# Up projection: product 2 of two neighbouring pairs as seven half-size products, and the next pair's product 1 sooner

## The chip, the cores and the metric

The kernel runs on one core of one Trainium2 chip. Its time is the device time of one execution in microseconds (us); three executions of the kernel before gave a median of 2516.06 us. The core's engines work side by side, each with its own queue of instructions: PE (TensorE, matrix products; PEld is its weight load), DVE (VectorE), ACT (ScalarE), POOL (GpSimd, which here issues stores) and SP (SyncE, which issues loads). They wait for each other through semaphores. PSUM is the accumulator memory of PE, eight banks of 512 fp32 values per partition.

## The reference

Two layers. Each has an attention part with two groups of heads, an output projection with a residual, and a gated feed-forward part with a short convolution. The feed-forward part is where the change is:

```python
def conv_ffn(x, w_up, conv_w, conv_b, w_down):
    h = x @ w_up                       # (1040, 1024) @ (1024, 5632)
    L = h.shape[1]
    hp = jnp.pad(h, ((0, 0), (CONV_W - 1, 0), (0, 0)))
    hc = conv_b
    for j in range(CONV_W):            # CONV_W = 3
        hc = hc + hp[:, j:j + L] * conv_w[j]
    u, g = jnp.split(hc, 2, axis=-1)
    return (jax.nn.silu(g) * u) @ w_down
...
    h = h + conv_ffn(rms_norm(h, ffn_norm[i]), w_up[i], conv_w[i], conv_b[i], w_down[i])
```

There are 1024 tokens and 16 learned ones ahead of them, T = 1040. The up projection gives 22 blocks of 128 columns for u and as many for g; the down projection brings 2816 channels back to 1024. All is fp32.

## The kernel before

**Arithmetic.** Every fp32 operand is split into a high and a low part (hi, lo: hi is the value cast to fp32r, lo the rest), and a product is three matmuls, hi by hi, lo by hi and hi by lo, added in PSUM (mm3, lines 222 to 224). A weight operand of 128x512 is read from a raw buffer, cast by ACT (line 1072) and its low part made by DVE (line 1073).

**Block products.** The up projection goes by pairs j = 0 to 21: column block j of u and of g together. The 1024 rows of the weights are cut in two halves, the tokens in two halves of 520 (layer 0) or 516 (layer 1), and the two column blocks make a 2 x 2 block product with seven block products instead of eight (Winograd's form of Strassen's scheme). The weights' blocks are A11, A12 (u), A21, A22 (g); S1, S2 and two more are sums and differences of them made by DVE (line 1055); the tokens' operands X[1] to X[7] are made once per layer. Product 2 is A12 by X[2] and goes into the u half t0 alone. One block product is 4 tiles of 128 rows, two pieces of 260 (258) columns and three matmuls each, 24 matmuls.

**PSUM and results.** A product accumulates in a tile of two banks; four tags p0 to p3 take the eight banks, and place() says which product goes where. Product 2 of j > 4 uses p3. evacuate() brings each result to SBUF: ACT copies it (line 1264) or DVE adds it to what is there (line 1263), into hu (for u) and hg (for g). After product 3 come the convolution, conv() (ACT Identity line 1252, two DVE steps on line 1256, for g and for u), Silu on ACT (line 1283), the product of both halves on DVE (line 1287) and the store of the result, actd, by POOL (line 1288). hu, hg and the convolution's results (cv) live in slots of SBUF of 1040 values; slots come from one list, in the order in which they were given back, and a slot that a store reads is free when that store has landed.

**Order.** PE's order in the feed-forward part is written out by hand; the order on the other engines comes from a scheduler in the framework. The products' order is the list seq; steady, it is (j,2), (j,6), (j,5), (j,7), (j+1,1), (j,4), (j,3). The weight operand of a product is built four products ahead (AHEAD, ensure()), in rings of three buffers for even and three for odd places in seq, so that a buffer is written again for the sixth product after. Towards the end of the stage (the last pair) the first operands of the down projection are prepared, on request of ffn_up through its argument during_last: loads of actd (st), high part by ACT and low part by DVE (lines 336 and 337: ah, al, and x for blocks of its own seven-product scheme with sums on line 1381), and weight tiles (lines 189 and 191).

The order before is this in the code:

```python
for j in range(3, NFF - 1):
    seq += ([(j, 2)] if j > 4 else []) + [(j, 6), (j, 5), (j, 7), (j + 1, 1), (j, 4), (j, 3)]
seq += [(NFF - 1, p) for p in (6, 5, 7, 2, 4, 3)]
```

## Time and profile before

| what | value |
| --- | --- |
| median of 3 executions (lowest to highest) | 2516.06 us (2515.10 to 2519.42) |
| the profiled execution's own time | 2518.04 us |
| its span in the profile | 2516.3 us |
| clock granted to PE | 0.996 |
| PE busy | 2477.9 us, 98% |
| DVE busy | 1767.2 us, 70% |
| ACT busy | 1272.9 us, 51% |
| POOL busy | 385.3 us, 15% |
| HBM traffic | 177.29 MB read, 67.81 MB written |

The profile is of one execution. A group of instructions is given by its line in the kernel, engine and operation, with what it writes and reads (out<-in), its shape, how often it ran, the time that it was busy and the mean of one in ns, and the engine's idle time just before with what ended it. A row of the timeline has the start in us, the duration, then the same; in square brackets stands the idle time before it and what released it. A row of the waits says who waited for whom: us in total, times, longest. A duration reaches to the end of the instruction; the next one on the same engine can start a little sooner, so the distance of starts is the cost in a full queue. In the chain of work that ended last each step is what released the next.

### The profile page before, as it was taken

Reading aid. Unit: us, or ns where it says so; the run is one execution under the profiler, and the core shown is the slowest. Engines: PE = TensorE matmul, PEld = TensorE weight load, DVE = VectorE, ACT = ScalarE, POOL = GpSimd, SP = SyncE. Lnnn points to the kernel's source line nnn. Section 1 sums busy time; section 2 is a strip of 40 time slices with the busy share of each in tenths; the row PEclk is TensorE's granted clock in tenths of the full one; section 3 lists DMA queues with packets and bytes.
Section 4 is the critical chain, followed back from the end, with each engine's and each line's share of the span. In section 5 each row is a group of like instructions: output and inputs, shape, how many; then the busy total and the mean of one; then the engine's idle time right before and its main releaser. Section 6 shows DMA issues by size and latency. Waiting matters only on the chain.

```text
span 2516.3 us, 47049 instructions
## 1 busy us (share of the span) xinstructions
PE 2477.9 (98%) x18442; PEld 2383.8 (95%) x18442; DVE 1767.2 (70%) x3523; ACT 1272.9 (51%) x2733; POOL 385.3 (15%) x567
## 2 busy tenths in 40 slices
PE   9999999999999999999999999999999999999998
PEld 8999999999999999999999899999999999997786
DVE  8656777769877777853666666777798777787535
ACT  7346666636544445631443566665464444455312
POOL 2023433210000000100211234331100000001002
PEclk9999999999999999999999999999999999999999
DMA  3232134343322224763312222143433222258722
GB/s 133 67 88 74 44 92 133 118 130 97 119 81 81 77 77 146 193 170 106 107 57 69 74 80 78 58 153 109 142 105 101 76 79 78 80 166 186 194 56 74
DMA packets 118542, 260.94 MB, mean 104 GB/s; under 512 B 14880, under 2 KB 32544, under 8 KB 118320
## 3 DMA queue, kind: packets, MB, share of 16 engines
q1 hardware_dynamic: 93984, 182.79, 23.5%
q0 software_dynamic: 22464, 72.84, 10.4%
q8 instruction: 144, 2.36, 0.4%
q10 hardware_dynamic: 1872, 2.31, 0.3%
q14 instruction: 78, 0.64, 0.1%
HBM read 177.29 MB, written 67.81 MB: 97 GB/s over the span
## 4 chain that ended last, share of the span: by engine, by line
PE 81%; DVE 10%; ACT 4%; DMA 2%; issue 2%; SPq 0%; POOL 0%; DVEq 0%; ACTq 0%; POOLq 0%
PE up L222 11%; PE up L224 11%; PE up L223 11%; PE mm L222 7%; PE mm L224 7%; PE mm L223 7%; PE down L222 5%; PE down L223 5%; PE down L224 5%; PE av L720 3%; PE tr L694 2%; DVE S L661 1%; PE S L658 1%; ACT P L673 1%; PE S L659 1%
## 5 line engine op out<-in xcount | busy, mean ns | idle before, releaser
L222 PE MATMUL up<-x,hi 128*128 128x260 f32 (+1 forms) x2464 | 696.6, 283 | 0.0
L224 PE MATMUL up<-x,hi 128*128 128x260 f32 (+1 forms) x2464 | 695.9, 282 | 0.7 <-DVE x L1097 0.7
L223 PE MATMUL up<-x,lo 128*128 128x260 f32 (+1 forms) x2464 | 696.3, 283 | 0.0
L224 PEld LDWEIGHTS up<-x,hi 128*128 128x128 f32 x2464 | 465.3, 189 | 1.1 <-DVE x L1097 1.1
L222 PEld LDWEIGHTS up<-x,hi 128*128 128x128 f32 x2464 | 464.5, 189 | 0.4 <-DVE hu L1263 0.2
L223 PEld LDWEIGHTS up<-x,lo 128*128 128x128 f32 x2464 | 464.5, 189 | 0.1
L1073 DVE TENSOR_TENSOR lo<-raw,hi 128x512 fp32r<-128x512 f32 x364 | 247.7, 685 | 173.0 <-ACT hi L1072 172.7
L222 PE MATMUL mm<-xh,hi 128*128 128x348 f32 (+4 forms) x1056 | 362.7, 343 | 0.0
L224 PE MATMUL mm<-xl,hi 128*128 128x348 f32 (+4 forms) x1056 | 339.8, 322 | 0.0
L223 PE MATMUL mm<-xh,lo 128*128 128x348 f32 (+4 forms) x1056 | 339.4, 321 | 0.0
L1072 ACT CAST hi<-raw 128x512 fp32r<-128x512 f32 x364 | 223.6, 620 | 128.1 <-PE up L224 84.5
L222 PEld LDWEIGHTS mm<-xh,hi 128*128 128x128 f32 x1056 | 199.5, 189 | 5.2 <-issue 4.6
L223 PEld LDWEIGHTS mm<-xh,lo 128*128 128x128 f32 x1056 | 199.5, 189 | 0.7 <-issue 0.7
L224 PEld LDWEIGHTS mm<-xl,hi 128*128 128x128 f32 x1056 | 198.3, 188 | 0.4 <-issue 0.3
L189 ACT CAST hi<-raw 128x512 fp32r<-128x512 f32 (+2 forms) x168 | 97.4, 581 | 176.0 <-PE down L224 97.0
L223 PE MATMUL down<-ah,lo 128*128 128x260 f32 (+1 forms) x528 | 168.6, 319 | 0.4 <-DVE lo L191 0.3
L224 PE MATMUL down<-al,hi 128*128 128x260 f32 (+1 forms) x528 | 168.5, 319 | 0.0
L222 PE MATMUL down<-ah,hi 128*128 128x260 f32 (+1 forms) x528 | 168.2, 319 | 0.0
L673 ACT ACTIVATE P<-S,m 116x460 f32<-116x460 f32 (+2 forms) x224 | 124.8, 561 | 71.2 <-DVE m L661 67.6
L337 DVE TENSOR_TENSOR PT<-tr,PT 116x464 fp32r<-116x464 f32 (+3 forms) x240 | 122.8, 514 | 46.9 <-ACT PT L336 45.3
L1055 DVE TENSOR_TENSOR raw<-raw,raw 128x512 f32<-128x512 f32 x198 | 129.4, 684 | 17.2 <-DMA raw<-in_wd_dram 16.5
L1288 POOL DMA_DIRECT2D actd<-cv x44 | 23.6, 535 | 756.9 <-DVE cv L1287 735.9
(289 smaller groups left out, 5623.8 us busy)
## 6 DMA issues: line engine op xcount, KB each, us to landing
raw<-in_wm_dram SPq DMA_DIRECT2D x330, 256.0 KB, 2.7
raw<-in_wd_dram SPq DMA_DIRECT2D x64, 256.0 KB, 3.6
actd<-cv POOLq DMA_DIRECT2D x22, 520.0 KB, 3.0
actd<-cv POOLq DMA_DIRECT2D x22, 512.0 KB, 2.9
cb<-cd SPq DMA_DIRECT2D x16, 520.0 KB, 4.1
st<-actd SPq DMA_DIRECT2D x14, 520.0 KB, 4.9
st<-actd SPq DMA_DIRECT2D x14, 512.0 KB, 4.6
kA<-kA SPq DMA_DIRECT2D x24, 260.0 KB, 3.9
```

Of the source, the lines that this page charges most:

```text
L189: nc.scalar.copy(hi[:, :n, :], raw[:, :n, :])
L222: nc.tensor.matmul(ps, wh, xh[:, c0:c0 + n], start=first, stop=False, skip_group_check=more)
L223: nc.tensor.matmul(ps, wl, xh[:, c0:c0 + n], start=False, stop=False, skip_group_check=more)
L224: nc.tensor.matmul(ps, wh, xl[:, c0:c0 + n], start=False, stop=last, skip_group_check=more)
L337: nc.vector.tensor_tensor(out=lo, in0=src, in1=hi.bitcast(F32), op=ALU.subtract)
L658: nc.tensor.matmul(S[:rows, :n], q["qA"][e][:, qs], q["kA"][e][:, c0:k1], start=True, stop=False)
L673: nc.scalar.activation(P[:rows, :n], S[:rows, :n], AF.Exp, scale=-1.0, bias=m[:rows, nch - 1:nch], accum_out=(den if nch == 1 else d3[:row ...
L694: nc.tensor.transpose(tr[:w, 3 - j, :rows], P[:rows, o:o + w], id_)
L720: nc.tensor.matmul(av[:, a:b], w.rearrange("p a b -> p (a b)"), x, start=(t == ts[0] and part == 0 and i == 0), stop=(t == last and i == 1))
L1055: nc.vector.tensor_tensor(out=q[out][:, :nk, :], in0=q[a][:, :nk, :], in1=q[b][:, :nk, :], op=op)
L1072: nc.scalar.copy(hi[:, :nk, :], src[:, :nk, :])
L1073: nc.vector.tensor_tensor(out=lo[:, :nk, :], in0=src[:, :nk, :], in1=hi[:, :nk, :].bitcast(F32), op=ALU.subtract)
```

## The change

From j = 6 on the pairs are taken two by two, (6,7) to (20,21): eight such couples in each layer. The two products 2 of a couple, A12 of j and of j+1 by the same token operand X[2], are themselves taken as a 2 x 2 block product: the 512 rows in two halves of 256, the tokens in the two pieces of 260 (258), the column blocks j and j+1 (written (j, SUB + i) in seq, m1 to m7). It takes seven half-size products instead of eight; each is 2 tiles of 128 rows, one piece and three matmuls, 6 matmuls.

- Their weight operands are half as wide (128x256): A12's halves, or sums of them that DVE makes (sub_operand), then split as others are. Raw weights of j and j+1 are both loaded for the first of them (block_raws).
- Their token operands are halves of X[2] and four new ones, Y[7], Y[6], Y[5], Y[4], made by second_level(): two additions on DVE of the high and low parts of X[2], four sums of quarters and four splits, one step with each product of j = 4 and 5 in the list. Y takes four slots until m4 of j = 20 is done; X[2] is given back then too, and during_last is called there once.
- They accumulate in two tiles of one bank, s0 (m1, m6, m7, m4) and s1 (m2, m5, m3). The accumulation goes on in place: after each product but the last of a bank the running sum is added by DVE to the quarter of hu it belongs to (sub_evacuate, 128x260), and the next product is added to it in the bank. The banks are those of tag p3, which PsumLast closes at the first couple and opens again after m4 of j = 20.
- The order of a couple is m1, m2, (j,6), m6, (j+1,1), m5, (j,7), (j,5), m7, (j,4), m3, (j,3), m4, (j+1,6), (j+1,5), (j+1,7), (j+2,1), (j+1,4), (j+1,3): product 1 of j+1 stands before (j,7).
- Operand 3 is written into S2's buffer instead of A12's, in both layers and in the down projection's blocks, which use the same function.

Matmuls fall by 96 in the whole program. DVE gets 18 small operations per couple and loses two splits and two additions of a whole product.

```diff
...
 AHEAD = 4
+SUB = 20
 NSPLIT = 4
 N_DMA_SUM = 5
+FIRST_SUB = 6
 WARM = 12
...
         return pool.tile(shape, dtype, tag=tag, name=name, bufs=bufs)
+class PsumLast:
+    def __init__(self, tc, pool, name):
+        self.tc, self.pool, self.name, self.n, self.own = tc, pool, name, 0, None
+    def turn(self):
+        self.close()
+        self.own = self.tc.tile_pool(name=f"{self.name}_{self.n}", bufs=1, space=PSUM, reuse_waits="tile")
+        self.last = self.own.__enter__()
+        self.n += 1
+    def close(self):
+        if self.own is not None:
+            self.own.__exit__(None, None, None)
+            self.own = None
+    def tile(self, shape, dtype, tag, name, bufs):
+        return (self.pool if tag in ("p0", "p1", "p2") else self.last).tile(shape, dtype, tag=tag, name=name, bufs=bufs)
+    def __enter__(self):
+        self.turn()
+        return self
+    def __exit__(self, *e):
+        self.close()
...
             return self.up_split(src, fw, odd)
-        return self.block_operand(self.wm[lyr, M_UP + 2 * j], self.wm[lyr, M_UP + 2 * j + 1], 4, j, p, fw, raws, odd, j < N_DMA_SUM)
-
-    def block_operand(self, u, g, nk, j, p, fw, raws, odd, by_dma=False):
+        src = lambda j: (self.wm[lyr, M_UP + 2 * j], self.wm[lyr, M_UP + 2 * j + 1], 4, j)
+        if p > SUB:
+            self.block_raws(*src(j), fw, raws)
+            self.block_raws(*src(j + 1), fw, raws)
+            return self.sub_operand(raws[j], raws[j + 1], p - SUB, fw, odd)
+        return self.block_operand(*src(j), p, fw, raws, odd, j < N_DMA_SUM)
+    def sub_operand(self, q, r, m, fw, odd):
+        A, B = q["A12"], r["A12"]
+        lo, hi = slice(0, 2), slice(2, 4)
+        tt = lambda out, a, b, op: self.nc.vector.tensor_tensor(out=out, in0=a, in1=b, op=op)
+        if m == 6:
+            q["s"] = fw.tile([128, 4, 128], F32, tag="raw2", name="raw2")
+            tt(q["s"][:, lo, :], B[:, lo, :], B[:, hi, :], ALU.add)
+            tt(q["s"][:, hi, :], q["s"][:, lo, :], A[:, lo, :], ALU.subtract)
+        elif m == 7:
+            tt(q["s"][:, lo, :], A[:, lo, :], B[:, lo, :], ALU.subtract)
+        elif m == 3:
+            tt(q["s"][:, hi, :], A[:, hi, :], q["s"][:, hi, :], ALU.subtract)
+        src, at = {1: (A, lo), 2: (A, hi), 3: (q.get("s"), hi), 4: (B, hi), 5: (q.get("s"), lo),
+                   6: (q.get("s"), hi), 7: (q.get("s"), lo)}[m]
+        return self.up_split(src[:, at, :], fw, odd, 2)
+    def block_raws(self, u, g, nk, j, fw, raws, by_dma=False):
...
                 nc.gpsimd.dma_start(q["S1"][:], g[:, 4:8, :], accum_op=ALU.add)
+    def block_operand(self, u, g, nk, j, p, fw, raws, odd, by_dma=False):
+        nc = self.nc
+        self.block_raws(u, g, nk, j, fw, raws, by_dma)
         q = raws[j]
...
         elif p == 3:
-            combine("A12", "A12", "S2", ALU.subtract)
-        src = q[{1: "A11", 2: "A12", 3: "A12", 4: "A22", 5: "S1", 6: "S2", 7: "A21"}[p]]
+            combine("S2", "A12", "S2", ALU.subtract)
+        src = q[{1: "A11", 2: "A12", 3: "S2", 4: "A22", 5: "S1", 6: "S2", 7: "A21"}[p]]
         return self.up_split(src, fw, odd, nk)
...
         seq += [(2, 6), (2, 5), (2, 7), (3, 1), (2, 4), (2, 3)]
-        for j in range(3, NFF - 1):
+        for j in range(3, FIRST_SUB):
             seq += ([(j, 2)] if j > 4 else []) + [(j, 6), (j, 5), (j, 7), (j + 1, 1), (j, 4), (j, 3)]
-        seq += [(NFF - 1, p) for p in (6, 5, 7, 2, 4, 3)]
+        for j in range(FIRST_SUB, NFF, 2):
+            m = lambda i: (j, SUB + i)
+            seq += [m(1), m(2), (j, 6), m(6), (j + 1, 1), m(5), (j, 7), (j, 5), m(7), (j, 4), m(3), (j, 3)]
+            seq += [m(4), (j + 1, 6), (j + 1, 5), (j + 1, 7)] + ([(j + 2, 1)] if j + 2 < NFF else [])
+            seq += [(j + 1, 4), (j + 1, 3)]
...
-        st = {}
+        st, building = {}, []
...
+        Y = {}
+        def second_level():
+            at0, at1 = slice(0, n), slice(n, W)
+            t = [half_slot("t") for _ in range(2)]
+            def whole(i):
+                return lambda: nc.vector.tensor_tensor(out=t[i].t[:, :, :W], in0=X[2][0][i].t[:, :, :W].bitcast(F32),
+                                                       in1=X[2][1][i].t[:, :, :W].bitcast(F32), op=ALU.add)
+            b11, b12, b21, b22 = (x.t[:, :, at] for x in t for at in (at0, at1))
+            def make(m, out, a, b, op):
+                def f():
+                    nc.vector.tensor_tensor(out=out, in0=a, in1=b, op=op)
+                def g():
+                    Y[m] = y = s.get(F32R, f"y{m}", (128, 4, 260))
+                    self.split(y.t[:, 0:2, :n], y.t[:, 2:4, :n], out)
+                return [f, g]
+            return [whole(0), whole(1), *make(7, b12, b22, b12, ALU.subtract), *make(6, b11, b12, b11, ALU.add),
+                    *make(5, b22, b22, b11, ALU.subtract), *make(4, b21, b21, b11, ALU.subtract),
+                    lambda: s.put(*t)]
+        def sub_moving(m):
+            if m in Y:
+                return [(Y[m].t[:, k, :], Y[m].t[:, 2 + k, :]) for k in range(2)], 0
+            i, c0 = {1: (0, 0), 2: (1, 0), 3: (1, n)}[m]
+            return [(X[2][0][i].t[:, k, :], X[2][1][i].t[:, k, :]) for k in range(2)], c0
+        def sub_evacuate(j, m):
+            bank = sub_bank(m)
+            to, c = {1: (j, 0), 2: (j, 0), 6: (j, 1), 3: (j, 1), 5: (j + 1, 1), 7: (j + 1, 1), 4: (j + 1, 0)}[m]
+            o = st[to]["u"][:, halves[0] + c * n:halves[0] + c * n + n]
+            nc.vector.tensor_tensor(out=o, in0=st[j]["s"][bank][:, :n], in1=o, op=ALU.add)
+        sub_bank = lambda m: 0 if m in (1, 6, 7, 4) else 1
         def evacuate(j, p):
+            if p > SUB:
+                sub_evacuate(j, p - SUB)
+                return
             q = st[j]
...
                 s.put(u, g)
-                del st[j]
+                if "s" not in q:
+                    del st[j]
             q.setdefault("done", set()).add(p)
...
                 before[i]()
+            if (j, p) == (4, 6):
+                building = second_level()
+            if j in (4, 5) and (j, p) != (4, 1) and building:
+                building.pop(0)()
+            if p == SUB + 1:
+                while building:
+                    building.pop(0)()
             q = st.setdefault(j, {})
+            if p > SUB:
+                m = p - SUB
+                if m == 1:
+                    if j == FIRST_SUB:
+                        pp.turn()
+                    q["s"] = [pp.tile([128, 512], F32, tag=f"s{b}", name="sub", bufs=1) for b in range(2)]
+                xs, c0 = sub_moving(m)
+                first = m in (1, 2, 5)
+                for k in range(2):
+                    self.mm3(q["s"][sub_bank(m)][:, :n], ops[i][k], xs[k], c0, n, first and k == 0, k == 1, not first)
+                ops[i] = None
+                evacuate(j, p)
+                if (j, m) == (NFF - 2, 4):
+                    for x in X.pop(2):
+                        s.put(*x)
+                    s.put(*Y.values())
+                    pp.turn()
+                    during_last(2)
+                continue
             bank, first = {2: "y", 5: "x", 3: "x"}.get(p, "a"), p in (1, 2, 5)
...
                 ids = s.add(fp, 6, f"e{lyr}_")
-                with tc.tile_pool(name=f"ups{lyr}", bufs=1, space=PSUM, reuse_waits="tile") as pp, \
-                        tc.tile_pool(name=f"up{lyr}", bufs=7, reuse_waits="tile") as fw:
+                with tc.tile_pool(name=f"up{lyr}", bufs=7, reuse_waits="tile") as fw, \
+                        tc.tile_pool(name=f"ups{lyr}", bufs=1, space=PSUM, reuse_waits="tile") as up, \
+                        PsumLast(tc, up, f"last{lyr}") as pp:
                     tail, down = self.ffn_down(lyr, pp, fw, halves, acts, X, ids)
...
```

## The prediction

> **What bounds the kernel now.** I read the page first: its busy line, its chain and its costliest groups.
>
> ```profile
> span 2516.3 us, 47049 instructions
> ...
> PE 2477.9 (98%) x18442; PEld 2383.8 (95%) x18442; DVE 1767.2 (70%) x3523; ACT 1272.9 (51%) x2733; POOL 385.3 (15%) x567
> ...
> PE 81%; DVE 10%; ACT 4%; DMA 2%; issue 2%; SPq 0%; POOL 0%; DVEq 0%; ACTq 0%; POOLq 0%
> ...
> L222 PE MATMUL up<-x,hi 128*128 128x260 f32 (+1 forms) x2464 | 696.6, 283 | 0.0
> ...
> L1073 DVE TENSOR_TENSOR lo<-raw,hi 128x512 fp32r<-128x512 f32 x364 | 247.7, 685 | 173.0 <-ACT hi L1072 172.7
> ```
>
> TensorE is busy nearly all the time and carries 81% of the chain; the up matmuls are three groups of 2464 like the one shown, one per line L222 to L224. So a matmul taken out is worth its time, if nothing else becomes late. Next I read the waits of TensorE over the two layers' feed-forward parts (568 to 1090 us, then 1812 to 2400 us) and the busy time of each engine by stretch (columns: sum, PE, PEld, DVE, ACT, POOL busy, clock, DMA share, GB/s).
>
> ```profile
> PE up L224 <- DVE x L1097: 0.2, 1, 0.2
> ...
> PE down L222 <- DVE dg L1444: 2.7, 1, 2.7
> ...
> PE up L224 <- DVE x L1097: 0.5, 1, 0.5
> PE down L223 <- DVE lo L191: 0.3, 1, 0.3
> ```
>
> ```profile
> 568.00:655.00 87.00, 86.81 (x714) 86.15 (x713) 86.75 (x128) 52.03 (x83) 5.74 (x8) 1.00 0.39 115
> 655.00:675.00 20.00, 20.00 (x170) 20.00 (x169) 15.63 (x21) 11.31 (x17) 0.53 (x1) 1.00 0.28 94
> 715.00:755.00 40.00, 40.00 (x337) 40.00 (x337) 29.46 (x39) 19.39 (x28) 1.06 (x2) 1.00 0.23 80
> 1000.00:1020.00 20.00, 20.00 (x170) 20.00 (x169) 20.00 (x20) 13.84 (x19) 1.41 (x2) 1.00 0.63 193
> ```
>
> The first wait row is layer 0's, the others are layer 1's. In the up projection TensorE waits 0.2 and 0.5 us in all, at its start; one more wait, 0.3 us, comes on the third weight tile of the down projection. VectorE (DVE) is different by stage: full up to 655 us, 29.46 of 40 us in a steady pair, and full again from 1000 us on, where the down projection's operands are prepared. These last 16 us of the stage I call the tail. So the change is judged in three places: the steady pair, the pairs j=4 and 5 where new operands are built, and the tail.
>
> **The saving.** The rate of TensorE comes from a DVE instruction that recurs once per j, the add of product 3 into hu.
>
> ```profile
> 715.70 0.69 DVE L1263 TENSOR_TENSOR hu<-up,hu 128x520 f32<-128x520 f32 x1
> 716.31 1.29 DVE L1256 SCALAR_TENSOR_TENSOR cv<-hg,vec,cv 128x1038 f32<-128x1038 f32 x1
> 717.52 0.68 DVE L1073 TENSOR_TENSOR lo<-raw,hi 128x512 fp32r<-128x512 f32 x1
> 718.12 1.29 DVE L1256 SCALAR_TENSOR_TENSOR cv<-hu,vec,cv 128x1039 f32<-128x1039 f32 x1
> 719.33 0.69 DVE L1263 TENSOR_TENSOR hu<-up,hu 128x520 f32<-128x520 f32 x1
> 719.94 1.28 DVE L1256 SCALAR_TENSOR_TENSOR cv<-hu,vec,cv 128x1038 f32<-128x1038 f32 x1
> 721.15 0.68 DVE L1073 TENSOR_TENSOR lo<-raw,hi 128x512 fp32r<-128x512 f32 x1
> 721.75 1.23 DVE L1287 TENSOR_TENSOR cv<-cv 128x1040 f32<-128x1040 f32 x1
> 722.91 0.68 DVE L1073 TENSOR_TENSOR lo<-raw,hi 128x512 fp32r<-128x512 f32 x1
> ...
> 735.77 0.69 DVE L1263 TENSOR_TENSOR hu<-up,hu 128x520 f32<-128x520 f32 x1
> ```
>
> ```profile
> 2000.65 0.69 DVE L1263 TENSOR_TENSOR hu<-up,hu 128x516 f32<-128x516 f32 x1
> ...
> 2041.06 0.69 DVE L1263 TENSOR_TENSOR hu<-up,hu 128x516 f32<-128x516 f32 x1
> ```
>
> From 715.70 to 735.77 lie 7 products of 24 matmuls: 20.07 us for 168, 0.1195 us each. In layer 1, 2000.65 to 2041.06 is two periods: 40.41 / 336 = 0.1203 us. A pair had 2 x 24 matmuls for product 2 and now has 7 x 6 = 42 of the same width. Six fewer per pair, 8 pairs per layer: 48 x 0.1195 + 48 x 0.1203 = **11.5 us** less TensorE time, 0.72 us per pair. It is a saving only if TensorE stays dense.
>
> **DVE in a steady pair.** The small operations (128x256 and 128x260) have a near row at the kernel's end, with starts a third of a us apart:
>
> ```profile
> 2501.48 0.41 DVE L1611 TENSOR_TENSOR h<-mm,h 128x256 f32<-128x256 f32 x1
> 2501.82 0.40 DVE L311 TENSOR_TENSOR r<-r,sq 128x256 f32<-128x256 f32 x1
> 2502.15 0.41 DVE L1611 TENSOR_TENSOR h<-mm,h 128x256 f32<-128x256 f32 x1
> ```
>
> One reads PSUM, one does not; both take 0.335 us from start to start. The 520-wide ones take 0.61 (715.70 to 716.31), the splits 0.60, the convolution's steps 1.21, the product of both halves 1.16. Removed per pair: two splits and two 520-wide adds, 2.4 us. Added: seven half splits, four combinations and seven evacuations, 18 x 0.335 = 6.0 us. So DVE has 29.46 - 2.4 + 6.0 = 33.1 us of work in a pair of 40.1 - 0.7 = 39.4 us, 84%: it fits on average. ScalarE (ACT) loses two casts and gets seven half ones: between +0.9 and +3.1 us (a half one at half or all of a whole one's 0.62) on 19.39, which hides.
>
> The Trainium skill, "VectorE: DVE Perf Modes", section on the TRN2 errata, speaks against this: every DVE operation pays a fixed cost, so work is to be cut in pieces of 512 elements or more, and an fp32 tensor_tensor of N takes (N+151)/0.96 ns. By it a small one is 0.43 us and a pair's DVE work an estimated 34.7 us, which still fits. The rows above do not agree: they start 0.335 us apart. By the rule the margin of 0.9 us that the next part finds would be some 0.6, and the third rival below a little likelier (I would give it 0.18); the sum would be the same.
>
> **The tightest place.** What can hurt is the order. I walk the DVE queue as the changed program has it, with t=0 at the start of product m1 and, as now (715.70 against the product's end near 715.0), the hu add of the pair before at 0.7: hu add to 1.3, convolution g to 2.5, evacuation of m1 to 2.9, convolution u to 4.1, half split for m5 to 4.4, convolution u to 5.6, evacuation of m2 to 6.0, product of both halves to 7.1, split for (j,7) to 7.8. TensorE's times are sums of 0.72 per half product and 2.87 per whole one, in the new order m1, m2, (j,6), m6, (j+1,1), m5, (j,7): m6 starts at 4.3 in the bank that m1's evacuation must have left (2.9), m5 at 7.9 in that of m2 (6.0), and (j,7) uses its low part at 8.7 (7.8). Margins 1.4, 1.9 and **0.9 us**. All others are wider: (j,5) 8.4 against 11.6, m7 9 against 14.3, m3 10.3 against 17.9, (j,3) 15.2 against 18.6, (j+1,5) 22.4 against 25.1. The lead with which operands are built falls from 5 x 2.87 = 14.3 us to 7.9 us where half products stand in the ring of six, which the loads keep to since they are issued some 8 us ahead and land in 2.7 (below). ACT's Silu, which the product of both halves needs, is ready early:
>
> ```profile
> 716.43 1.26 ACT L1252 ACTIVATE cv<-hu,vec 128x1040 f32<-128x1040 f32 x1 [0.78 <-DVE hu L1263]
> 717.69 1.08 ACT L1283 ACTIVATE cv<-cv 128x1040 f32<-128x1040 f32 x1
> ...
> raw<-in_wm_dram SPq DMA_DIRECT2D x330, 256.0 KB, 2.7
> actd<-cv POOLq DMA_DIRECT2D x22, 512.0 KB, 2.9
> ```
>
> With one cast moved between them Silu ends at about t=4.4, before 6.0. I take 0 us here. The bounds: 0, and, if the run-up of nine operations were 0.2 us longer each, (1.8 - 0.9) x 16 = 14 us. Nothing in these bounds is a gain, since TensorE cannot be denser than without a wait.
>
> (j+1,1) is moved ahead of (j,7): its operand is ready by then, its copy to hu(j+1) needs a slot that the store of two pairs before left long ago (2.9 us landing). Slots in rotation fall from 11 to 7; stores are some 14 us old when their slot is taken. SP issues as many loads and POOL as many stores as before; the loads of j+1 go out sooner, along with those of j, and none waits for a buffer that a later product holds. Combination 3 written into S2 and not into A12 is the same operation and frees a load buffer sooner. The two banks handed to the half products are those of tag p3, whose last product, (5,2), ended a whole period earlier; when they are handed back after m4 of j=20, the next to use them is the down projection, so both turns cost 0.
>
> **j=4 and 5.** The second-level operands cost DVE two adds of 1040 (1.16) and eight operations of 520 (0.61), 7.2 us per layer, and ACT four casts. They lie over two periods, in which DVE has 20 - 15.63 = 4.4 us (655 to 675) and then 5.3 us idle; 9.7 us holds 7.2. Before 655 there is none, so a lag is possible: 0 to 1 us per layer, I take 0.1, because operands here are still 14 us ahead.
>
> **The tail.** Here something new is queued:
>
> ```profile
> 2250.59 1.22 DVE L337 TENSOR_TENSOR al<-st,ah 128x1024 fp32r<-128x1024 f32 x1
> 2251.73 1.21 DVE L1287 TENSOR_TENSOR cv<-cv 128x1024 f32<-128x1024 f32 x1
> ...
> 2268.34 0.55 DVE L191 TENSOR_TENSOR lo<-raw,hi 128x384 fp32r<-128x384 f32 x1
> ```
>
> ```profile
> 2253.24 0.53 POOL L1288 DMA_DIRECT2D actd<-cv  x1 [22.32 <-DVE cv L1287]
> ...
> 2258.72 0.80 SPq L1333 DMA_DIRECT2D st<-actd  x2
> ...
> 2259.89 0.39 PE L222 MATMUL down<-ah,hi 128*128 128x512 f32 x1
> ...
> 2268.94 0.50 PE L223 MATMUL down<-ah,lo 128*128 128x512 f32 x1 [0.33 <-DVE lo L191]
> ```
>
> E is the end of the up projection, 2259.89 here. Before, the last activation operand (al, 2250.59) is made ahead of the product for j=20 (2251.73). In the changed program its high part takes a slot that only the store of j=20 frees, in both layers: it comes after that product, its store, and the landing. The store is issued at E-6.7 (2253.24) and lands 2.9 us later by the median row, or 5.5 us later if the load that follows it (2258.72) waited for it alone: E-3.8 to E-1.2. ACT's copy takes about 1.2 us (its 1040-wide operation above took 1.26), so DVE can make al from E-2.6 to E. Without the wait DVE would reach it at about E-1.9. So it waits 0 to 1.9 us, and behind it in DVE's queue stand x6, x2, x5, four convolution steps and the low part of the third weight tile, which TensorE already waits 0.33 us for (2268.94). From the product of j=20 on DVE has also 0.5 us more work before that tile. Loss: 0.5 to 2.4 us in layer 1, 0 to 2.4 in layer 0. I take the middle of both, 1.4 + 1.2 = 2.6 us, having no row for the landing in that stretch that is nearer to one end. The down projection after it has the same work; its waits (dg, 2.7) recur, with slots in another order, which I put at 0, bounds -2 and +2 us per layer.
>
> **Sum.** -11.5 + 0 + 2 x 0.1 + 2.6 = -8.7 us against the profiled execution's 2518.0 (span 2516.3): 2509.3. The median of the runs, 2516.06, is 2.0 lower, so 2507.4 us.
>
> **Rivals.** First, the store of j=20 lands early and DVE gets over the tail: -11.5 and no loss, 2504.6. For: 2.9 us landing. Against: DVE is already full there (20.00 of 20). Second, the tail and the down projection take most back: two tails of 2.4 and 2 us in each layer's down phase, with 1 us lag at j=4 and 5 in each, is 10.8; 2515. Third, on the other side: DVE holds TensorE up once in each pair, at the low part for (j,7). It decides when the nine operations before it take over 0.9 us longer than walked; every us beyond is 16 us. To be slower by 5 us it needs 0.9 + (8.7 + 5)/16 = 1.8 us; with 2.5 us, 2516.1 - 8.7 + 16 x 1.6 = 2533. For: the longest run of DVE work without a gap, and evacuations now block banks. Against: rows of all its operations are known to a few hundredths.
>
> **How the numbers follow.** The main case, 2505.5 to 2511, has 0.54, no loss in the tail 0.14, the gain eaten (2511 to 2520) 0.17, DVE bound (above 2521) 0.15. 0.2% is 5 us, about what a measurement here tells from no change: faster 0.54 + 0.14 = 0.68, same 0.17, slower 0.15. The range 2503.5 to 2517 leaves out the last case and the end of the third; the likeliest one's own is 2505.5 to 2511.
>
> **What would show it.** Right: hu adds of one pair to the next 39.4 us apart in layer 0; no wait of the up matmuls on L1263's or the new add's banks; TensorE waiting 1 to 3 us for the third weight tile's low part in each layer; DVE near 33 us per pair. Wrong: a wait that recurs 16 times, on a low part or on an evacuation; a wait of ACT on a store in the steady pairs; or a span under 2504.

## The result, and the profile after

The changed kernel takes 2522.08 us (median of 21 executions, 2518.86 to 2526.03); the kernel before, beside it on the same chip, takes 2518.25 us (21 executions, 2514.13 to 2522.28). The ratio is 1.0016 with a 95% interval of 1.0009 to 1.0023: 3.8 us slower where 8.7 us less was forecast, and above the forecast's range of 2503.5 to 2517. The profiled execution of the changed kernel is the quickest of its 21 (2518.86 us), so its trace stands only 0.8 us above the one of before (2518.04 us).

The page of the changed kernel, the lines that answer to those of before:

```profile
span 2516.6 us, 47358 instructions
...
PE 2467.1 (98%) x18346; PEld 2371.2 (94%) x18346; DVE 1846.3 (73%) x3767; ACT 1302.9 (52%) x2821; POOL 385.6 (15%) x567
```

TensorE does 96 matmuls fewer and is busy 10.8 us less (2477.9 before), yet the span is the same. So the saving was made, and turned into idle time of TensorE. Where that idle time lies is seen by stage; the rows of the kernel before for the same stretches stand in the prediction. The first row below is the start of the up projection, the second j=4 and 5, the third a steady stretch, the fourth the tail (changed kernel, busy time by stretch: sum, PE, PEld, DVE, ACT, POOL, clock, DMA share, GB/s):

```profile
568.00:655.00 87.00, 86.06 (x708) 85.31 (x707) 86.85 (x128) 52.61 (x83) 5.75 (x8) 1.00 0.39 114
655.00:675.00 20.00, 20.00 (x170) 20.00 (x169) 19.96 (x28) 12.33 (x19) 0.53 (x1) 1.00 0.38 120
715.00:755.00 40.00, 40.00 (x337) 40.00 (x336) 34.00 (x54) 21.24 (x35) 1.07 (x2) 1.00 0.25 82
1000.00:1020.00 20.00, 18.36 (x152) 17.94 (x150) 20.00 (x21) 13.57 (x18) 1.41 (x2) 1.00 0.44 117
```

In the steady stretch TensorE has no gap (40.00 of 40) with DVE at 34.00 of 40, and none at j=4 and 5, where DVE is full (19.96 of 20). It lost 0.75 us at the start (86.81 before) and 1.64 us in the tail (20.00 before). The next rows are the waits of TensorE in the changed kernel. The first six are layer 0 (560 to 1009 us, then 1005 to 1225 us), the last four layer 1 (1810 to 2252 us, then 2244 to 2470 us); the three waits of layer 0's up projection recur in layer 1 with 0.8, 0.7 and 0.5 us and are not shown again:

```profile
PE up L253 <- DVE lo L1130: 0.8, 1, 0.8
PE up L252 <- ACT hg L1365: 0.7, 1, 0.7
PE up L252 <- ACT hi L1129: 0.2, 1, 0.2
...
PE down L252 <- DVE dg L1572: 2.9, 1, 2.9
PE down L252 <- ACT du L1573: 2.5, 2, 1.5
PE down L253 <- DVE lo L221: 1.3, 1, 1.3
...
PE up L254 <- DVE x L1154: 0.5, 2, 0.3
...
PE down L252 <- DVE dg L1572: 2.9, 1, 2.9
PE down L252 <- ACT du L1573: 2.7, 2, 1.6
PE down L253 <- DVE lo L221: 1.4, 1, 1.4
```

The waits of the down projection of layer 0 before; in layer 1 they were 2.7 and 1.0 us, and 0.3 us for the third weight tile:

```profile
PE down L222 <- DVE dg L1444: 1.9, 1, 1.9
PE down L222 <- ACT du L1445: 1.0, 1, 1.0
```

No wait recurs with the pairs; each is paid once or twice in a layer. Those of the up projection are new, but for the 0.5 us on x in layer 1, which the kernel before has too. Their rows in the timeline of the changed kernel, first the start of product (1,6), then that of (21,4):

```profile
591.88 0.38 PE L252 MATMUL up<-x,hi 128*128 128x260 f32 x1 [0.16 <-ACT hi L1129]
593.04 0.39 PE L253 MATMUL up<-x,lo 128*128 128x260 f32 x1 [0.78 <-DVE lo L1130]
...
1003.33 0.28 PE L254 MATMUL up<-x,hi 128*128 128x260 f32 x1
1004.29 0.39 PE L252 MATMUL up<-x,hi 128*128 128x260 f32 x1 [0.68 <-ACT hg L1365]
```

The two starts 1003.33 and 1004.29 are 0.96 us apart, where matmuls follow each other at 0.12: product (21,4) goes on in the bank that (21,7) has just left, and waits for its copy. Before, (21,2) stood between them.

To sum up the stages, the next table has the time from the first up matmul to the last one (up), and from there to the first matmul behind the down projection (down), starts taken from the timeline. In layer 0 of the changed kernel the three starts are 568.81, 1009.98 and 1225.27 us; before, 568.17, 1012.83 and 1223.42 us. The experiments' rows are used below; each is of one profiled execution.

| kernel | up, layer 0 | down, layer 0 | up, layer 1 | down, layer 1 |
| --- | --- | --- | --- | --- |
| before | 444.66 | 210.59 | 448.08 | 206.53 |
| changed | 441.18 | 215.29 | 445.28 | 208.12 |
| e1_s2_only | 445.49 | 211.30 | 449.13 | 203.27 |
| e2_no_s2 | 440.16 | 219.11 | 443.85 | 209.27 |
| e3_m4_late | 440.94 | 214.04 | 445.59 | 209.15 |
| e4_slots | 441.20 | 217.40 | 443.79 | 206.66 |
| e8_last_plain | 441.00 | 211.20 | 444.95 | 206.66 |
| e9_last_plain_no_s2 | 439.75 | 210.58 | 443.71 | 210.91 |
| e10_last_only | 445.16 | 221.47 | 449.43 | 211.39 |
| e11_pin | 440.25 | 212.23 | 444.80 | 207.59 |
| e12_pin_before | 444.34 | 211.46 | 448.00 | 202.91 |
| e14_pump_order | 440.17 | 219.04 | 445.91 | 215.83 |

In the profiled executions the up projection became 3.48 + 2.80 = 6.3 us shorter instead of 11.5, and the down projection 4.70 + 1.59 = 6.3 us longer. What one profile is worth is seen in e1 and e12, the kernel before with one small edit each: their down projection takes 211.3 and 211.5 us in layer 0, and 203.3 and 202.9 in layer 1, where the profile of before has a stretch at half clock and they have none. Beside these two the changed kernel loses some 5 us in layer 1 as well, which fits its median better than its trace does.

### The profile page after: what moved, and what is told of

Same layout as the page of the kernel before. It is cut to its first block, busy times and chain, and to the rows that moved or that the text cites. A ratio compares the mean times of both kernels' runs of the same rounds, so it can differ in the third digit from the quotient of the medians.

```text
span 2516.6 us, 47358 instructions
## 1 busy us (share of the span) xinstructions
PE 2467.1 (98%) x18346; PEld 2371.2 (94%) x18346; DVE 1846.3 (73%) x3767; ACT 1302.9 (52%) x2821; POOL 385.6 (15%) x567
## 4 chain that ended last, share of the span: by engine, by line
PE 46%; issue 33%; DVE 12%; ACT 4%; DMA 3%; POOL 1%; SPq 0%; POOLq 0%; DVEq 0%; ACTq 0%
PE mm L252 7%; PE mm L254 7%; PE mm L253 7%; PE down L252 4%; PE down L253 4%; PE down L254 4%; PE av L750 3%; PE tr L724 2%; DVE S L691 1%; PE S L688 1%; PE wo L252 1%; PE wo L254 1%; PE wo L253 1%; PE S L689 1%; ACT P L703 1%
## 5 line engine op out<-in xcount | busy, mean ns | idle before, releaser
L252 PE MATMUL up<-x,hi 128*128 128x260 f32 (+1 forms) x2208 | 625.1, 283 | 2.0 <-ACT hg L1365 1.4
L253 PE MATMUL up<-x,lo 128*128 128x260 f32 (+1 forms) x2208 | 624.1, 283 | 1.6 <-DVE lo L1130 1.6
L254 PE MATMUL up<-x,hi 128*128 128x260 f32 (+1 forms) x2208 | 623.4, 282 | 0.5 <-DVE x L1154 0.5
L252 PEld LDWEIGHTS up<-x,hi 128*128 128x128 f32 x2208 | 416.4, 189 | 3.1 <-ACT hg L1365 1.8
L253 PEld LDWEIGHTS up<-x,lo 128*128 128x128 f32 x2208 | 416.5, 189 | 2.0 <-DVE lo L1130 1.9
L254 PEld LDWEIGHTS up<-x,hi 128*128 128x128 f32 x2208 | 417.0, 189 | 0.9 <-DVE x L1154 0.9
L1130 DVE TENSOR_TENSOR lo<-raw,hi 128x512 fp32r<-128x512 f32 (+1 forms) x444 | 268.4, 618 | 93.7 <-ACT hi L1129 92.4
L1129 ACT CAST hi<-raw 128x512 fp32r<-128x512 f32 (+1 forms) x444 | 246.9, 566 | 160.9 <-PE up L254 92.5
L1112 DVE TENSOR_TENSOR raw<-raw,raw 128x512 f32<-128x512 f32 x198 | 135.0, 686 | 8.4 <-DMA raw<-in_wd_dram 6.3
```

The lines of the kernel that those rows point to most:

```text
L252: nc.tensor.matmul(ps, wh, xh[:, c0:c0 + n], start=first, stop=False, skip_group_check=more)
L253: nc.tensor.matmul(ps, wl, xh[:, c0:c0 + n], start=False, stop=False, skip_group_check=more)
L254: nc.tensor.matmul(ps, wh, xl[:, c0:c0 + n], start=False, stop=last, skip_group_check=more)
L1112: nc.vector.tensor_tensor(out=q[out][:, :nk, :], in0=q[a][:, :nk, :], in1=q[b][:, :nk, :], op=op)
L1129: nc.scalar.copy(hi[:, :nk, :], src[:, :nk, :])
L1130: nc.vector.tensor_tensor(out=lo[:, :nk, :], in0=src[:, :nk, :], in1=hi[:, :nk, :].bitcast(F32), op=ALU.subtract)
```

## The experiments

Theory A: each couple saves what its matmuls cost, and waits that are paid once in a layer (the start, the last couple, the down projection) take it back. Theory B: each couple saves less, because its half products or their evacuations hold TensorE up a little every time. The experiments undo one suspect each.

### e1_s2_only: the kernel before with combination 3 written into S2

```diff
-            combine("A12", "A12", "S2", ALU.subtract)
-        src = q[{1: "A11", 2: "A12", 3: "A12", 4: "A22", 5: "S1", 6: "S2", 7: "A21"}[p]]
+            combine("S2", "A12", "S2", ALU.subtract)
+        src = q[{1: "A11", 2: "A12", 3: "S2", 4: "A22", 5: "S1", 6: "S2", 7: "A21"}[p]]
```

> The kernel before with one part of the change alone: combination 3 is written into S2's buffer and not over A12. Theory A (the gain was eaten by waits paid once per layer, of which this buffer rule makes the one at the up projection's start, because it puts DVE's combination for product (1,6) behind operand building): the up matmuls wait about 1.0 us more per layer at (1,6), as in the changed kernel, and the time is 1 to 3 us longer than before. Theory B (each couple saves less than its matmuls, because DVE's small operations hold TensorE up or thin its stream out): this part has nothing to do with it, 0 us, no new wait at (1,6).

Measured: 2518.72 us against 2517.59, ratio 1.0006 (0.9996 to 1.0015). The waits of the up projection in this kernel, layer 0 (layer 1 has the same with 0.8 and 0.5):

```profile
PE up L223 <- DVE lo L1073: 0.8, 1, 0.8
PE up L222 <- ACT hi L1072: 0.2, 1, 0.2
```

They are the waits of the changed kernel at (1,6), made by these two lines alone, and the up projection is 0.83 and 1.05 us longer than before. The whole time does not tell 1.9 us from nothing here. What comes late is the combination for (1,6) on DVE, first in the kernel before, then in the changed one:

```profile
587.08 0.68 DVE L1055 TENSOR_TENSOR raw<-raw,raw 128x512 f32<-128x512 f32 x1
```

```profile
590.49 0.68 DVE L1112 TENSOR_TENSOR raw<-raw,raw 128x512 f32<-128x512 f32 x1
```

DVE is full there, and the combination stands 3.4 us later in its queue. That it does so follows from the rule for the buffer, since nothing else differs. A likely reason is in the code: the buffers for such sums (raw2) are seven, and by the time S2 of j=0 is made, A21, A22 and S1 of j=0 and 1 and this S2 fill them. Before, S2 of j=0 was free again as soon as it was split; with operand 3 to be written into it, it is kept, and S2 of j=1, which is the combination for (1,6), has to wait for another. The low part at 588.67 us ends at 589.35 in the changed kernel, shortly ahead of the combination. The trace does not say which buffer was taken, so this is argued and not shown.

### e2_no_s2: the changed kernel with combination 3 written into A12 again

```diff
-            combine("S2", "A12", "S2", ALU.subtract)
-        src = q[{1: "A11", 2: "A12", 3: "S2", 4: "A22", 5: "S1", 6: "S2", 7: "A21"}[p]]
+            combine("A12", "A12", "S2", ALU.subtract)
+        src = q[{1: "A11", 2: "A12", 3: "A12", 4: "A22", 5: "S1", 6: "S2", 7: "A21"}[p]]
```

> The changed kernel with combination 3 written over A12 as before. Theory A: the wait at (1,6) (1.4 us in layer 0, some 1.7 in layer 1) falls to nearly none, the time is 1 to 3 us shorter than that of the changed kernel. Theory B: no difference.

Measured: 2523.02 us against 2517.59, ratio 1.0023 (1.0013 to 1.0032); no gain over the changed kernel, so the expectation is missed. The up projection did become 1.02 and 1.43 us shorter and the wait at (1,6) is gone in both layers. But the order of DVE at the end of the stage changed as well. The wait on the third weight tile in this kernel, in layer 0; in layer 1 it is 1.7 us (1.3 and 1.4 in the changed kernel):

```profile
PE down L253 <- DVE lo L221: 3.2, 1, 3.2
```

And behind the 3.2 us wait TensorE was granted half its clock for 3.4 us (busy time by stretch; the number before the last two is the clock), this kernel first, then the changed one:

```profile
1015.00:1021.00 6.00, 2.81 (x24) 2.60 (x22) 6.00 (x7) 5.28 (x8) 1.60 (x3) 1.00 0.57 89
...
1021.00:1026.00 5.00, 4.99 (x29) 5.00 (x30) 5.00 (x5) 2.86 (x4) 0.69 (x2) 0.66 0.91 178
```

```profile
1021.00:1026.00 5.00, 5.00 (x44) 5.00 (x44) 5.00 (x6) 4.99 (x9) 1.43 (x2) 1.00 0.88 197
```

29 matmuls instead of 44 in the same 5 us. A stretch of 3.4 us at half clock costs some 1.7 us where TensorE has work all the time. This trace has two more of them in the down projections, behind the waits for dg, and the changed kernel's has none. So a rule for one buffer decides waits in two places, and what it takes at one it gives back at the other.

### e3_m4_late: in the last couple, m4 between (21,7) and (21,4)

```diff
-            seq += [m(4), (j + 1, 6), (j + 1, 5), (j + 1, 7)] + ([(j + 2, 1)] if j + 2 < NFF else [])
+            more = j + 2 < NFF
+            seq += ([m(4)] if more else []) + [(j + 1, 6), (j + 1, 5), (j + 1, 7)] + [(j + 2, 1) if more else m(4)]
```

> The changed kernel with m4 of the last couple moved from ahead of (21,6) to between (21,7) and (21,4), which use the same PSUM tile back to back in the changed kernel. Theory A: the wait of 0.8 us before (21,4) goes in both layers, up to 1.7 us shorter than the changed kernel, unless DVE, full there, gives it back at the third weight tile. Theory B: no difference.

Measured: 2520.37 us against 2517.59, ratio 1.0014 (1.0005 to 1.0024). The wait of 0.7 us on the copy of hg is gone. The up projection is no shorter in sum (440.94 and 445.59 us against 441.18 and 445.28). Later banks and operands now come late by about as much, as this row of the down projection of layer 1 shows in this kernel (with 0.5 more on ah and 0.5 on al):

```profile
PE down L252 <- DVE hu L1365: 0.8, 1, 0.8
```

The bank was the cause of that wait. Its 0.84 us per layer (0.96 - 0.12) was not had by this move; that m4, standing later, also gives back X[2] and the bank later would explain it, but was not tested.

### e4_slots: in the down projection, the slots of acts given back ahead of those that stores read

```diff
             if m == KD - 1:
-                s.put(*going)
-                going.clear()
                 for j in range(g0, g0 + ng):
                     s.put(*acts.pop(j))
+                s.put(*going)
+                going.clear()
```

> The changed kernel with the slots of the first down group's activation operands given back ahead of the slots of its three result buffers, so that the first du copies take a slot that TensorE has read and not one that a store reads. Theory A: the wait of 1.5 us for du at the start of the down blocks goes in both layers, 2 to 3 us shorter than the changed kernel, if no later copy takes the stored slots in its place. Theory B: no difference.

In the changed kernel the copies du wait for a store to land. Its rows on ACT, and the store's on POOL:

```profile
1053.09 0.59 ACT L1573 COPY du<-down 128x520 f32<-128x520 f32 x1 [5.41 <-DMA hm<-do]
```

```profile
1047.45 0.84 POOL L1665 DMA_DIRECT2D hm<-do  x1 [1.86 <-ACT do L1663]
```

From the store's issue to the copy lie 5.6 us. Before, the same copy waited for its product alone:

```profile
1050.78 0.59 ACT L1445 COPY du<-down 128x520 f32<-128x520 f32 x1 [1.22 <-PE down L224]
```

Measured: 2518.50 us against 2517.59, ratio 1.0004 (0.9995 to 1.0013), beside 1.0016 (1.0009 to 1.0023) of the changed kernel. The intervals overlap; the waits say it more plainly. du fell from 2.5 and 2.7 us to this in layer 0 and 1.2 us in layer 1, about what they were before:

```profile
PE down L252 <- ACT du L1573: 1.1, 1, 1.1
```

So the list of slots, in the order in which the changed up projection left it, hands the down projection slots whose stores have just gone out. That cost 1.4 and 1.5 us. In the table the down projection of layer 1 is shorter by that much (206.66 us against 208.12), that of layer 0 is longer (217.40 against 215.29): this trace has two stretches of 3.4 us at half clock there, from 1020.46 and 1129.69 us, and the changed kernel's has none.

### e8_last_plain and e9_last_plain_no_s2: the last couple as before

Both leave pairs 20 and 21 as they were before the change, with product 2 whole; seven couples are left in each layer. e9 also has combination 3 in A12, as e2.

```diff
-        for j in range(FIRST_SUB, NFF, 2):
+        for j in range(FIRST_SUB, NFF - 2, 2):
...
+        j = NFF - 2
+        seq += [(j, 2), (j, 6), (j, 5), (j, 7), (j + 1, 1), (j, 4), (j, 3)]
+        seq += [(j + 1, p) for p in (6, 5, 7, 2, 4, 3)]
...
-                if (j, m) == (NFF - 2, 4):
-                    for x in X.pop(2):
-                        s.put(*x)
+                if (j, m) == (NFF - 4, 4):
                     s.put(*Y.values())
                     pp.turn()
-                    during_last(2)
```

> The changed kernel with the last couple (20,21) of each layer computed as before, with two whole products 2 and the old order; the other seven couples stay. It gives up 2 x 0.72 us of saved matmuls. Theory A (waits paid once per layer, most of them from the end of the stage on): the waits before (21,4), for the third weight tile and for the first du copy shrink to those of the kernel before; the up projections keep about 10 us of saving less 2 us at (1,6): 2510 to 2513 us where the kernel before takes 2517.6. Theory B (each couple saves less than its matmuls): the time changes by nothing clear from the changed kernel's, 2520 to 2523 us.

> The same, and combination 3 written over A12 as before, so that the start of the stage keeps its old order too. Theory A: 2507 to 2511 us, that is about 14 us of saving for the pairs less small waits, 10.0 us of matmuls in all. Theory B: 2519 to 2523 us.

The figure of about 14 us in the second text is a slip: fourteen couples of 0.72 us are 10.0.

Measured: e8 2515.69 us against 2517.25, ratio 0.9995 (0.9986 to 1.0004); e9 2513.85 us against the same, ratio 0.9986 (0.9977 to 0.9995). Both miss theory A's range (2510 to 2513, 2507 to 2511) and lie well below theory B's. In e8 the third weight tile of layer 1 is waited for 2.9 us, so that wait did not shrink to that of the kernel before. In e9 the up projection is 4.91 and 4.37 us shorter than before, where seven couples at 0.72 are 5.0, and layer 0 has no wait of 0.1 us or more in it. So the couples save most of what their matmuls cost, and theory B does not account for the loss; the rate, worked out further down, leaves it some 0.06 us per couple in layer 0. In layer 0 the down projection is as long as before (210.58 and 210.59). What is missing in e9 lies in one place, the third weight tile of layer 1 (PE, then ACT, then DVE of this kernel):

```profile
2262.69 0.80 PE L253 MATMUL down<-ah,lo 128*128 128x512 f32 x1 [3.06 <-DVE lo L221]
```

```profile
2253.93 1.05 ACT L366 CAST x<-st 128x1024 fp32r<-128x1024 f32 x1 [3.77 <-DMA st<-actd]
```

```profile
2256.16 1.28 DVE L1320 SCALAR_TENSOR_TENSOR cv<-hg,vec,cv 128x1024 f32<-128x1024 f32 x1 [3.55 <-ACT cv L1316]
```

ACT stood 3.77 us at a cast for the down projection whose load had not landed; the convolution of j=21 was queued behind it, DVE waited 3.55 us for that, and the tile's low part came behind DVE's convolution steps. From 2261.95 us on, shortly before this wait ends, the clock was halved for 6.8 us:

```profile
2262.00:2270.00 8.00, 7.31 (x20) 5.78 (x21) 7.95 (x10) 6.56 (x10) 1.41 (x2) 0.58 0.97 209
```

### e10_last_only: the last couple alone, in a kernel with all other pairs as before

```diff
-FIRST_SUB = 6
+FIRST_SUB = 20
```

and combination 3 in A12, as in e2.

> The changed kernel, combination 3 over A12, with half-size products in the last couple (20,21) alone; the second-level operands are built at j = 4 and 5 and held as before. It saves 2 x 0.72 = 1.4 us of matmuls. Theory A: the waits of the last couple and of the down projection come whole, and the time is 5 to 9 us longer than that of the kernel before. Theory B: within 2 us of it.

Measured: 2535.70 us against 2517.25, ratio 1.0074 (1.0062 to 1.0087): 18.4 us slower, twice and more what was expected, for a couple that saves 0.72 us per layer in matmuls. The wait on the third weight tile in layer 0 (4.0 us in layer 1), and the clock after it:

```profile
PE down L253 <- DVE lo L221: 4.1, 1, 4.1
```

```profile
1025.00:1032.00 7.00, 6.44 (x30) 6.44 (x31) 5.59 (x7) 3.42 (x5) 1.24 (x2) 0.52 0.86 203
```

The down projection of layer 0 is 10.9 us longer than before. Its waits are 8.6 us in all (4.1, dg 3.0, du 1.5) against 2.9 before, so 5.7; half clock over 6.8 and 3.4 us takes 5.1 more; the sum is 10.8. The end of the stage is where the change costs, and the direction was as theory A says. The size was not: alone, the last couple costs twice what it costs behind the seven others (some 9 us, see e14), and why is open.

### e11_pin and e12_pin_before: the cast that stood in the way, held in its place

e11 is e9 with the copy that ACT had taken too early held to the order of the program. e12 is the same edit in the kernel before, to see what it is worth without the couples.

```diff
-                    self.split(h, l, src[:, :m, :W])
+                    if (k0, p) == (2, 2):
+                        self.tc.keep_in_program_order(nc.scalar.copy(h, src[:, :m, :W]))
+                        nc.vector.tensor_tensor(out=l, in0=src[:, :m, :W], in1=h.bitcast(F32), op=ALU.subtract)
+                    else:
+                        self.split(h, l, src[:, :m, :W])
```

> Seven couples, combination 3 over A12, and ACT's copy of the second operand block's x2 pinned behind the instruction that stands ahead of it in the program. In the run with seven couples the scheduler had put this copy ahead of the convolution of j = 21 in layer 1, where it waited 3.8 us for a load; DVE and the third weight tile were late by it, 3.1 us on TensorE, and the clock was halved for 6.8 us there (3.4 us lost). Theory A (late work once per layer at the end of the stage, of any origin, decides): that wait falls under 1 us and the time to 2507 to 2511 us. Theory C (the seven couples are worth 3 to 4 us and no more, the rest is lost somewhere that no single wait shows): 2512 to 2515 us.

> The kernel before with the same copy pinned, and nothing else: the control for the run beside it. There the copy stood behind the convolution already. Theory A: within 2 us of the kernel before. If the pin is good by itself, it is faster by more than 3 us, and the seven couples are credited with the rest only.

Measured: e11 2510.86 us against 2516.96, ratio 0.9977 (0.9968 to 0.9986); e12 2517.00 us against the same, ratio 1.0000 (0.9991 to 1.0008). The waits of e11 in the down projection of layer 0; layer 1 has only du and dg, 1.8 us each:

```profile
PE down L252 <- DVE dg L1576: 1.8, 1, 1.8
PE down L252 <- ACT du L1577: 0.8, 1, 0.8
PE down L253 <- DVE lo L221: 0.4, 1, 0.4
```

The wait of 3.1 us on the third tile is gone, and the kernel beats both the one before (by 6.1 us, within theory A's range) and the changed one. Its interval overlaps that of e9, so what the pin adds there rests on the wait that went more than on the times. In the kernel before the pin gives nothing. e11 is the change with 14 of its 16 couples and 10.0 of its 11.5 us of matmuls less.

### e14_pump_order: the last couple kept, its release of X[2] and Y and the call of during_last(2) moved behind (21,7)

On top of e2:

```diff
                 if (j, m) == (NFF - 2, 4):
-                    for x in X.pop(2):
-                        s.put(*x)
-                    s.put(*Y.values())
                     pp.turn()
-                    during_last(2)
...
                 during_last(p)
+                if p == 7:
+                    for x in X.pop(2):
+                        s.put(*x)
+                    s.put(*Y.values())
+                    during_last(2)
```

> All eight couples, combination 3 over A12, and in the last pair the preparation of the down projection goes on at the places where the kernel before had them: X[2] and Y are given back, and the call for product 2 made, after (21,7) and not after m4 of j = 20. It asks why the last couple costs 9 us where it should save 1.4. Theory A1 (the earlier call puts DVE and ACT work of the down projection ahead of what TensorE needs next): the third weight tile's wait (3.3 and 1.9 us in the run with eight couples and A12) falls under 1 us in both layers; with the halved clock that follows it gone too, 2514 to 2519 us. Theory A2 (DVE is full there, and the last couple's small operations make it late in any order): the waits stay, 2520 to 2524 us.

Measured: 2529.04 us against 2517.38, ratio 1.0048 (1.0034 to 1.0062). The waits on the third tile fall from 3.2 and 1.7 us to 0.9 and 1.3, and others grow, most of all this one in layer 1:

```profile
PE down L252 <- ACT du L1574: 5.0, 2, 3.8
```

Neither reading of the expectation holds as it stands. When the first operands of the down projection are asked for does move the wait on the third tile, but asking later makes the operands behind it late. Which order would suit the last couple stays open, and so does the full cause of its price: it is some 9 us between e9 (2513.85) and e2 (2523.02), which differ in that couple and in what goes with it (the release of X[2] and Y, the call of during_last), where its matmuls save 1.4.

## Why the prediction was wrong, point by point

In short: the saving per couple was right, and the terms put at 0 were not. The down projection came out 4.7 and 1.6 us longer, the start of the up projection 0.9 and 2.2 us, and the last couple's own order cost 0.8 us in each layer.

**Right.** The rate (what the prediction calls a pair there is a couple, two values of j): the hu adds of the changed kernel recur after 757.51 - 718.07 = 39.44 us in layer 0 and 2045.99 - 2006.27 = 39.72 us in layer 1 (forecast 39.4; 40.41 before in layer 1).

```profile
718.07 0.69 DVE L1364 TENSOR_TENSOR hu<-up,hu 128x520 f32<-128x520 f32 x1
...
738.38 0.42 DVE L1356 TENSOR_TENSOR hu<-sub,hu 128x260 f32<-128x260 f32 x1
738.72 1.29 DVE L1317 SCALAR_TENSOR_TENSOR cv<-hu,vec,cv 128x1039 f32<-128x1039 f32 x1
...
757.51 0.69 DVE L1364 TENSOR_TENSOR hu<-up,hu 128x520 f32<-128x520 f32 x1
...
2006.27 0.69 DVE L1364 TENSOR_TENSOR hu<-up,hu 128x516 f32<-128x516 f32 x1
...
2045.99 0.69 DVE L1364 TENSOR_TENSOR hu<-up,hu 128x516 f32<-128x516 f32 x1
```

A small evacuation costs 0.34 us from start to start (738.38 to 738.72), as the price of 0.335 had it. (By the Trainium skill, "VectorE: DVE Perf Modes", section on the TRN2 errata, it would be 0.43: the duration in the row, 0.42, agrees, the distance of the starts does not.) DVE has 34.00 us of 40, which is 33.5 in 39.44 (forecast 33.1), and the tightest place, at (j,7), cost nothing. The third rival, DVE as the bound in each pair, did not happen. The lag at j=4 and 5 did not show either. Over seven couples TensorE's own starts say the same a little less well for layer 0: product m1 of j=6 to that of j=20 takes 972.58 - 696.22 = 276.36 us, 39.48 per couple, where product 2 of the same pairs took 40.13 before, so 0.65 us less and not 0.72; in layer 1 it is 39.69 after 40.40, 0.71 less.

**Right in size, and the mechanism in one layer only: the tail.** The wait on the third weight tile was forecast at 1 to 3 us per layer, and 2.6 us of loss in both; it is 1.3 and 1.4, and measured by the distances of the starts 1.29 + 1.06 = 2.4 us more than before. The prediction had al, the last low part of an activation operand, wait for the store of j=20. The first three rows are DVE in layer 0 of the changed kernel, the last two ACT and DVE in layer 1:

```profile
1006.23 1.23 DVE L1509 TENSOR_TENSOR t<-st 128x1040 f32<-128x1040 f32 x1
1007.38 1.23 DVE L367 TENSOR_TENSOR al<-st,ah 128x1040 fp32r<-128x1040 f32 x1
...
1019.74 0.55 DVE L221 TENSOR_TENSOR lo<-raw,hi 128x384 fp32r<-128x384 f32 x1
...
2257.07 1.05 ACT L366 CAST ah<-st 128x1024 fp32r<-128x1024 f32 x1 [1.54 <-DMA actd<-cv]
...
2258.16 1.23 DVE L367 TENSOR_TENSOR al<-st,ah 128x1024 fp32r<-128x1024 f32 x1 [0.37 <-ACT ah L366]
```

In layer 0 the store was no part of it: al follows its predecessor without a gap, and DVE is busy 20.00 of the 20 us from 1000 on. In layer 1 it was, in part: the store went out at 2253.13 us, ACT waited 1.54 us for it to land, and DVE then 0.37 us for ACT, a third of the 1.06. The rest is DVE's queue, which gains less than TensorE does: counted from the first up matmul, the up projection of layer 0 ends 3.48 us sooner than before, and the tile's low part (1019.74 us, 1021.27 before) is reached only 2.17 us sooner.

**Wrong: "Combination 3 written into S2 and not into A12 is the same operation and frees a load buffer sooner."** It is the same operation, but with it the combination for (1,6) stands 3.4 us later in a full DVE queue: 0.8 to 1.4 us in each layer by e1 and e2. The step looked at the buffer that comes free sooner, and not at the one that is then kept longer, nor at what DVE's order makes of it.

**Wrong by omission: the last pair's order.** The prediction walked the couple's order bank by bank only for the steady pair. In the last couple there is no (22,1) to stand between (21,7) and (21,4), and (21,2) is gone from there: 0.84 us in each layer.

**Wrong: the down projection "which I put at 0, bounds -2 and +2 us per layer".** It came out at the bad end. du waits 1.5 us more in layer 0 and 1.7 in layer 1, by the order of the slots (e4), and dg 1.0 and 0.2 more. In layer 0 dg is a matter of DVE's order, of which the prediction had nothing. In the changed kernel a low part al goes ahead of the addition of dg:

```profile
1128.06 1.24 DVE L367 TENSOR_TENSOR al<-st,ah 128x1040 fp32r<-128x1040 f32 x1
1129.21 0.69 DVE L1572 TENSOR_TENSOR dg<-down,dg 128x520 f32<-128x520 f32 x1
```

Before, the addition came first (1127.93 us, al at 1128.53), and so it does in e3 and e9, where the wait is 1.6 and 1.7 us. "Slots in rotation fall from 11 to 7" was judged for the pairs alone, where it was harmless; the list that is left behind was not followed into the next stage.

**The sum in its own terms.** Up projection, layer 0: -5.7 for the matmuls, +0.9 at (1,6), +0.8 at (21,4), together -4.0; measured -3.48, and the couples' 0.65 in place of 0.72 is the 0.5 us between. Layer 1: -5.8 for the matmuls, +0.8 at (21,4), and a start that is 2.2 us longer: from the first up matmul to product (5,2) it takes 109.55 us where it took 107.37. Of these 2.2 us 1.2 are at (1,6); most of the rest goes where TensorE waits for the operands x (L1154) earlier in the start, which the prediction left as it was and no experiment explains. Together -2.8; measured -2.80. Down projection: in layer 0 the waits account for 1.3 + 1.5 + 1.0 = 3.8 of 4.7 us, and 0.9 stays open; in layer 1 for 1.1 + 1.7 + 0.2 = 3.0, less 1.7 for a stretch at half clock that only the execution before had there (below), against 1.59 measured. This is the second rival, "the gain eaten", which had 0.7 us less than before and was still some 4.5 us too low.

**Not weighed at all: the clock.** By the traces the change costs 0.8 us, by the medians 3.8. Over the changed kernel's 21 executions time falls as the granted clock rises (correlation -0.74, about 1.3 us for 0.001); their mean clock is 0.9960, and the profiled one has 0.998. (Not every kernel shows it: over e11's 11 executions, at 0.996 to 0.998, the correlation is +0.1.) That accounts for some 2.6 of the 3.2 us between the profiled execution and the median. The kernel before has a mean of 0.9969 over the 31 executions beside e1 to e4. So typical executions of the changed kernel lose about 1 us more to the clock, which its longer waits at the end of the stages would explain; with a profile of one execution that link is argued and not shown.

## What to carry to other kernels

A saving per iteration is the easy part of such a sum: read the steady stretch, see whether every engine fits, multiply. What decides a change of half a per cent is what is paid once per stage: walk the first and the last iteration bank by bank and queue by queue in the changed order, and follow the lists (slots, buffers) that the stage hands on into the next one. Where a scheduler orders the queues, a rule for one buffer moves instructions in places that it does not name, so test such an edit alone; and where an optimisation hurts only at the seam, as here, leaving it out of the last iteration can be worth more than the iteration's saving.

## What the runs showed of the hardware that was not expected

Waits of TensorE of some 2 to 4 us are dearer than they look. In several runs a stretch of half clock begins at the end of one: at 3.2 us in e2, 3.1 us in e9, 4.1 us in e10, and in the kernel before at the wait of 2.7 us for dg:

```profile
2373.00:2376.40 3.40, 3.19 (x8) 2.51 (x9) 1.89 (x3) 0.29 (x1) 0.85 (x1) 0.52 0.81 261
```

It lasts 3.4 us, or twice that (6.8 in e9 and e10), and adds 1.7 us for each 3.4. It does not follow every such wait: the changed kernel's profile has waits of 2.9 us for dg in both layers and full clock after them. The Trainium skill, "TensorE: Matmul & The Clock Gate", section "HAM oscillation — how this bites in real kernels", gives the rule that TensorE should not idle for more than some 3.4 us. The traces here agree with the length of the stretch, but not with that bound, for 2.7, 3.1 and 3.2 us were already enough, and 1.8 us in e11; the measurement decides.

What sets the two kinds of wait apart is where they fall. In each trace the half-clock stretches start at whole multiples of 3.4133 us from each other: in the kernel before at 38.42, 458.26, 1700.71 and 2373.14 us, which are 123, 364 and 197 steps. Cut by this grid, the twelve traces agree between 20 and 2490 us: every step at full clock in which TensorE idled 2.4 us or more is followed by half clock (11 of them), none with 1.61 us or less is, and between 1.62 and 1.88 us both occur (21 are followed by it, 9 are not); no step lies between. The wait of 2.9 us for dg in the changed kernel, from 1127.08 us, is cut at 1128.80 into 1.7 and 1.2 us, that in layer 1 at 2374.67 into 1.5 and 1.4. So a wait of 1.8 us that fills half of a step can cost 1.7 us more, and a wait of 2.9 us across a border nothing.

A store's landing can be a hidden wait far from the store: 5.6 us from the issue of hm<-do to the copy that needed its slot. Stores differ, too: those of do, which add to what lies in HBM, take 6.8 us to land by the median row of the changed kernel, those of actd, as large (520 KB), 3.0 us.
